# Seven block products instead of eight in the down products, and none in the first gate and up product of a layer

## The chip, the core and the metric

The kernel runs on one core of one Trainium2 chip. The core has TensorE (matrix products, PE in the rows), VectorE (DVE), ScalarE (ACT), GpSimd (POOL) and SyncE (SP, which issues the loads), and each runs its own instructions in order. The metric is the device time of one execution in microseconds, as the median of several runs.

## What is computed

Two layers of a transformer block on 256 tokens of width 2048, in float32. Each layer normalises x, runs three mixers (a gated recurrence, a differential attention and a latent attention), adds their projection to x, and then runs a gated feed-forward part of width 5632, which the change is about:

```python
h = rmsnorm(x, g_ffn[l])
x = x + (jax.nn.silu(h @ w_gate[l]) * (h @ w_up[l])) @ w_down[l]
```

with `w_gate`, `w_up` of 2048 x 5632 and `w_down` of 5632 x 2048. At the end stands one more `rmsnorm`.

## The kernel before

**Precision.** Each float32 operand is split into a high part, rounded to the format that TensorE multiplies in one pass (`F32R`), and a low part, the rest. A product takes three matmuls (`mm3`, lines 232 to 236): high x high, high x low, low x high. For weights, ScalarE makes the high part from the raw tile (L228) and VectorE the low part (L229), in `load_split`. Raw tiles (`wraw`) have six buffers of 128x1024; high and low parts (`whi`, `wlo`) have three each.

**Feed-forward.** The 5632 hidden columns are taken in eleven blocks f of 512, in three groups (0 to 3, 4 to 7, 8 to 10). For each block, `gate_up` computes gate and up for both halves of the tokens (t = 0, 1), and a step called `hidden`, which runs between the matmuls of whatever comes next, transposes the result on TensorE and splits it into `hTh` and `hTl`. After a group, two down products (cg = 0, 1, each of 1024 output columns) multiply the group's hidden activations by `w_down` and add to x. They are written with the general `gemm`: one k-tile of 128 rows and 1024 columns at a time, 12 matmuls each, four banks.

**Seven products.** `gate_up` goes over the 16 k-tiles in eight pairs. A pair is a 2x2 block problem: two token halves, two k-tiles, and gate and up. The first five pairs (`NORD = 5`) are plain: 2 x 2 x 2 = 8 block products, 24 matmuls. The last three pairs use a scheme with seven block products (21 matmuls). It needs sums of the left blocks (`xSh`, `xSl`, built once per layer by `build_xS`) and, per pair, sums of the weight blocks: V and W, four subtractions of 128x512 on VectorE (L340 to L343), which are then split like the weights G (gate) and U (up) themselves (L338, L339, L344 to L349). In the plain pairs the parts go to `whi` and `wlo`; in the seven pairs *all* parts go to two sets in the arena, a large scratch tile, so that the next product's first plain pairs can fill the three `whi` and `wlo` buffers meanwhile. The seven accumulators are C11, C22, C21, C12 and P1 (pool `acc`, five banks) and P5, P6, P7 (pool `aux`, three banks); at the end VectorE combines them (L360, L368, L369, L373, L375 to L378, L380).

**Order.** TensorE's order is that of the code. On VectorE, ScalarE and SP a scheduler orders the instructions ahead of time; whatever stands inside `tc.high_priority` is pulled forward as far as its inputs and buffers allow. A buffer of a pool is given to the next tile when the last reader of its old tile is through.

Of the kernel before, what the change touches and what calls it, by code (L numbers as in the profile page):

```python
# [16 lines left out]
ALU = mybir.AluOpType  # L17
# [20 lines left out]
NORD = 5  # L38
# [19 lines left out]
def body(ctx: ExitStack, tc: tile.TileContext, x_in, pos_in, pvec_in, lamv_in, cst_in, w_in, w_r, w_i, w_q_b,  # L58
# [27 lines left out]
    xSh = xt_p.tile([P, KD // 2 - NORD, 4, P], F32R, name="xSh")  # L86
    xSl = xt_p.tile([P, KD // 2 - NORD, 4, P], F32R, name="xSl")
# [52 lines left out]
    A_SET, SET = 64, 7168  # L140
# [157 lines left out]
    def gate_up(wg, wu, rs, sil):  # L298
# [4 lines left out]
        f_ = lambda v: v.bitcast(F32)  # L303
        C11, C22, C21, C12 = (acc() for _ in range(4))
        bank = {(0, 0): C11, (1, 1): C22, (0, 1): C21, (1, 0): C12}
        sub = {}
        u2, u3, o22 = (at(A_U + i * 512, 512) for i in range(3))
        tt = nc.vector.tensor_tensor

        def xp(k, t):  # L310
            return xTh[:, k, t * P:(t + 1) * P], xTl[:, k, t * P:(t + 1) * P]

        for p in range(NORD):
            ks = (2 * p, 2 * p + 1)
            hl = [load_split(w[2 * p * P:(2 * p + 2) * P], 2, (512,)) for w in (wg, wu)]
            for s, t in ((0, 0), (1, 1), (0, 1), (1, 0)):
                hi, lo = hl[s]
                for j, k in enumerate(ks):
                    mm3(bank[s, t], xp(k, t), (hi[:, j], lo[:, j]), p == 0 and j == 0,
                        (s, t) == (1, 1) and p == NORD - 1 and j == 1)  # L320
            yield
        with tc.high_priority(offset=AHEAD):
            nc.scalar.copy(o22, C22)
        P1 = acc()
        P5, P7, P6 = (aux() for _ in range(3))
        n = KD // 2
        for p in range(NORD, n):
            ks = (2 * p, 2 * p + 1)
            a = A_SET + p % 2 * SET
# [3 lines left out]
            gh, gl = at(a, 2, 512), at(a + 1024, 2, 512)  # L333
            uh, ul = at(a + 2048, 512), at(a + 2560, 512)
            vh, vl = at(a + 3072, 2, 512), at(a + 4096, 2, 512)
            wh, wl = at(a + 5120, 2, 512), at(a + 6144, 2, 512)
            with tc.high_priority(offset=AHEAD):
                nc.scalar.copy(fl(gh), fl(G))  # L338
                nc.scalar.copy(uh, U[:, 1])  # L339
# [5 lines left out]
                tt(ul, U[:, 1], f_(uh), ALU.subtract)  # L345
# [4 lines left out]
            first, end = p == NORD, p == n - 1  # L350
            q = p - NORD
            S = [(xSh[:, q, i], xSl[:, q, i]) for i in range(4)]
            mm3(P1, xp(ks[0], 0), (gh[:, 0], gl[:, 0]), first, end)
            if end:
                with tc.high_priority(offset=AHEAD):
                    nc.scalar.copy(sil[1], P1)
            mm3(C11, xp(ks[1], 0), (gh[:, 1], gl[:, 1]), False, end)
            if end:
                with tc.high_priority(offset=AHEAD):
                    tt(sil[0], sil[1], C11, ALU.add)  # L360
                    nc.scalar.activation(sil[0], sil[0], AF.Silu, scale=rs[:, 0:1])
            mm3(C12, S[3], (uh, ul), False, end)
            mm3(P5, S[0], (vh[:, 0], vl[:, 0]), first, end)
            mm3(P7, S[2], (vh[:, 1], vl[:, 1]), first, end)
            mm3(P6, S[1], (wh[:, 0], wl[:, 0]), first, end)
            if end:
                with tc.high_priority(offset=AHEAD):
                    tt(u2, sil[1], P6, ALU.add)  # L368
                    tt(u3, u2, P7, ALU.add)  # L369
            mm3(C21, xp(ks[1], 1), (wh[:, 1], wl[:, 1]), False, end)  # L370
            if end:
                with tc.high_priority(offset=AHEAD):
                    tt(sil[1], u3, C21, ALU.add)  # L373
# [32 lines left out]
    def build_xT(gname, l, k):  # L406
        with tc.high_priority(offset=AHEAD):
# [4 lines left out]
            if gname == "g_ffn" and k // 2 >= NORD:  # L412
                build_xS(l, k, ps)
# [648 lines left out]
```

## Time and profile before

| | |
|---|---|
| median of 3 runs | 2117.31 us (2115.34 to 2117.53) |
| the profiled execution | 2116.37 us |
| its span, first to last instruction | 2114.5 us |
| TensorE busy | 2078.1 us, 10,104 matmuls and transposes |
| VectorE busy | 1539.4 us |
| ScalarE busy | 1132.4 us |
| DMA | 391.16 MB, mean 185 GB/s |
| TensorE waits for VectorE's split L229 | 13.6 us in 23 waits |

Busy times are sums over the span; a matmul's duration overlaps the next one's, so TensorE's pace is read from the starts of its instructions. "Idle before, releaser" in a row tells how long the engine had waited and what ended that.

### The profile page before, as it was taken

To read this page: it belongs to the slowest core of one execution; us is meant where nothing else is said; L and a number is where in the kernel's file an instruction comes from. 1 tells how busy PE (TensorE), PEld (TensorE's weight loads), DVE (VectorE), ACT (ScalarE), POOL (GpSimd) and SP (SyncE) were. 2 spreads that over 40 slices of the span, in tenths; PEclk is the share of its full clock that TensorE was granted. 3 is DMA by queue.
4 is the path that set the end of the run, shared out by engine and by line. 5 is a ranking of instruction groups with operands and counts; after the bars stand their busy time and mean duration, and the time that the engine had idled before them with its cause. 6 is when DMAs were issued, how large, how long until landed. Compare 5 with 4: busy or idle time off the path is not lost.

```text
span 2114.5 us, 26989 instructions
## 1 busy us (share of the span) xinstructions
PE 2078.1 (98%) x10104; PEld 1738.2 (82%) x10104; DVE 1539.4 (73%) x2115; ACT 1132.4 (54%) x1541; POOL 14.9 (1%) x32
## 2 busy tenths in 40 slices
PE   8999999999999999999999999999999999999998
PEld 7898887787888888887898998877888888888786
DVE  5775757898469884698565756589884788758885
ACT  5764655555345553455447546465553555535554
POOL 0000000000000000000000000000000000000000
PEclk9999999999999999999999999999999999999999
DMA  7664555565656655565565645556556655666563
GB/s 244 170 181 135 163 176 154 185 223 189 191 168 205 205 197 192 175 211 199 173 191 156 195 124 175 177 158 206 189 199 191 196 195 174 210 193 204 180 216 133
DMA packets 183219, 391.16 MB, mean 185 GB/s; under 512 B 18960, under 2 KB 36384, under 8 KB 182960
## 3 DMA queue, kind: packets, MB, share of 16 engines
q1 hardware_dynamic: 183040, 389.36, 58.1%
q8 instruction: 79, 1.29, 0.3%
q14 instruction: 52, 0.43, 0.1%
q0 software_dynamic: 48, 0.09, 0.0%
HBM read 387.30 MB, written 2.10 MB: 184 GB/s over the span
## 4 chain that ended last, share of the span: by engine, by line
PE 59%; DVE 25%; DMA 9%; issue 4%; ACT 2%; DVEq 0%; SPq 0%; POOLq 0%; ACTq 0%; POOL 0%
PE acc L235 18%; PE acc L236 18%; PE acc L234 18%; DVE wlo L229 7%; DMA wraw<-in_w_up 5%; DVE arena L344 2%; DMA wraw<-in_w_gate 2%; DVE wraw L341 2%; DVE arena L349 2%; DVE wraw L342 2%; ACT whi L228 2%; PE aux L393 1%; DVE wraw L343 1%; DVE wraw L340 1%; DVE arena L345 1%
## 5 line engine op out<-in xcount | busy, mean ns | idle before, releaser
L229 DVE TENSOR_TENSOR wlo<-wraw,whi 128x1024 fp32r<-128x1024 f32 (+2 forms) x608 | 715.2, 1182 | 440.4 <-ACT whi L228 436.2
L228 ACT CAST whi<-wraw 128x1024 fp32r<-128x1024 f32 (+2 forms) x608 | 617.5, 1019 | 681.3 <-PE acc L236 532.7
L235 PE MATMUL acc<-wlo,xTh 128*128 128x512 f32 (+1 forms) x1200 | 467.1, 389 | 14.0 <-DVE wlo L229 13.6
L234 PE MATMUL acc<-whi,xTh 128*128 128x512 f32 (+1 forms) x1200 | 471.2, 393 | 0.0
L236 PE MATMUL acc<-whi,xTl 128*128 128x512 f32 (+1 forms) x1200 | 463.6, 386 | 0.0
L234 PE MATMUL acc<-whi,hTh 128*128 128x512 f32 (+1 forms) x992 | 388.9, 392 | 3.5 <-DVE arena L373 3.5
L236 PE MATMUL acc<-whi,hTl 128*128 128x512 f32 (+1 forms) x992 | 384.8, 388 | 0.0
L235 PE MATMUL acc<-wlo,hTh 128*128 128x512 f32 (+1 forms) x992 | 384.4, 388 | 0.0
L235 PEld LDWEIGHTS acc<-wlo,xTh 128*128 128x128 f32 x1200 | 225.5, 188 | 72.3 <-DVE wlo L229 30.0
L234 PEld LDWEIGHTS acc<-whi,xTh 128*128 128x128 f32 x1200 | 225.4, 188 | 44.0 <-ACT whi L228 0.5
L236 PEld LDWEIGHTS acc<-whi,xTl 128*128 128x128 f32 x1200 | 225.3, 188 | 44.0
L234 PEld LDWEIGHTS acc<-whi,hTh 128*128 128x128 f32 x992 | 186.4, 188 | 43.7 <-DVE arena L373 6.0
L236 PEld LDWEIGHTS acc<-whi,hTl 128*128 128x128 f32 x992 | 186.2, 188 | 38.0
L235 PEld LDWEIGHTS acc<-wlo,hTh 128*128 128x128 f32 x992 | 186.4, 188 | 36.2
L234 PE MATMUL acc<-xTh,whi 128*128 128x256 f32 x384 | 111.1, 289 | 1.7 <-ACT whi L228 1.2
L235 PE MATMUL acc<-xTl,whi 128*128 128x256 f32 x384 | 108.8, 283 | 1.9 <-DVE xTl L403 1.9
L236 PE MATMUL acc<-xTh,wlo 128*128 128x256 f32 x384 | 108.6, 283 | 0.5 <-DVE wlo L229 0.5
L348 ACT CAST arena<-wraw 128x1024 fp32r<-128x1024 f32 x66 | 69.6, 1054 | 61.4 <-DVE wraw L343 61.0
L346 ACT CAST arena<-wraw 128x1024 fp32r<-128x1024 f32 x66 | 69.5, 1053 | 49.8 <-DVE wraw L341 49.8
L344 DVE TENSOR_TENSOR arena<-wraw,arena 128x1024 fp32r<-128x1024 f32 x66 | 80.6, 1222 | 14.9 <-ACT arena L338 14.8
L338 ACT CAST arena<-wraw 128x1024 fp32r<-128x1024 f32 x66 | 69.3, 1050 | 23.8 <-DMA wraw<-in_w_gate 23.5
L349 DVE TENSOR_TENSOR arena<-wraw,arena 128x1024 fp32r<-128x1024 f32 x66 | 80.7, 1222 | 0.2
(230 smaller groups left out, 2523.1 us busy)
## 6 DMA issues: line engine op xcount, KB each, us to landing
wraw<-in_w_gate SPq DMA_DIRECT2D x176, 512.0 KB, 4.3
wraw<-in_w_up SPq DMA_DIRECT2D x176, 512.0 KB, 4.6
wraw<-in_w_down SPq DMA_DIRECT2D x176, 512.0 KB, 4.5
wraw<-in_w_out SPq DMA_DIRECT2D x64, 512.0 KB, 3.8
wraw<-in_w_in SPq DMA_DIRECT2D x48, 512.0 KB, 4.2
wraw<-in_w_in SPq DMA_DIRECT2D x48, 384.0 KB, 3.2
wraw<-in_w_in SPq DMA_DIRECT2D x32, 416.0 KB, 3.4
arena<-in_w_in SPq DMA_DIRECT2D x16, 384.0 KB, 7.4
```

The source lines that it names most:

```text
L228: nc.scalar.copy(hi[:, :n], raw[:, :n])
L229: nc.vector.tensor_tensor(lo[:, :n], raw[:, :n], hi[:, :n].bitcast(F32), ALU.subtract)
L234: nc.tensor.matmul(ps, a[0], b[0], start=start, stop=False)
L235: nc.tensor.matmul(ps, a[0], b[1], start=False, stop=False)
L236: nc.tensor.matmul(ps, a[1], b[0], start=False, stop=stop)
L338: nc.scalar.copy(fl(gh), fl(G))
L341: tt(V[:, 1], U[:, 1], U[:, 0], ALU.subtract)
L342: tt(W[:, 0], U[:, 1], V[:, 0], ALU.subtract)
L344: tt(fl(gl), fl(G), f_(fl(gh)), ALU.subtract)
L346: nc.scalar.copy(fl(vh), fl(V))
L348: nc.scalar.copy(fl(wh), fl(W))
L349: tt(fl(wl), fl(W), f_(fl(wh)), ALU.subtract)
```

## The change

`gate_up` becomes `paired`, which takes the left operands (`part`, `sums`), the two weight matrices and a function for the read-out (`ev`) as arguments. `gate_up` calls it as before, except that the first block of a layer (f = 0) passes no seven pairs: all eight are plain, and its four banks are read directly. `down` is new: it calls `paired` with the two halves of 512 columns of a down product in the places of gate and up, and with the pairs of hidden k-tiles on the left. Of eight pairs, 3, 4 and 5 are done last and by seven products. The third group has six pairs: its cg = 0 takes none, its cg = 1 takes pairs 3 and 4 in layer 0, and in layer 1 it stays with `gemm`. `hidden` builds the sums of hidden activations for these pairs (`build_sums`), into 3072 columns of the arena. That room comes from the sets: only V and W keep their parts in the arena (two sets of 4096), and the parts of G and U of a seven pair go to `whi` and `wlo`. `hidden` starts one pair earlier.

```diff
+SEVEN_X, SEVEN_H = (5, 6, 7), (3, 4, 5)
...
-            gh, gl = at(a, 2, 512), at(a + 1024, 2, 512)
-            uh, ul = at(a + 2048, 512), at(a + 2560, 512)
-            vh, vl = at(a + 3072, 2, 512), at(a + 4096, 2, 512)
-            wh, wl = at(a + 5120, 2, 512), at(a + 6144, 2, 512)
+            gh, uh = (whl_p.tile([P, CHUNK], F32R, name="whi").rearrange("p (a b) -> p a b", a=2) for _ in range(2))
+            gl, ul = (whl_p.tile([P, CHUNK], F32R, name="wlo").rearrange("p (a b) -> p a b", a=2) for _ in range(2))
+            vh, vl, wh, wl = (at(A_SET + (i % 2 * 4 + m) * 1024, 2, 512) for m in range(4))
...
+    def down(w, c, hT, order, seven, done):
...
+        def add_x(t, g, *vs):
+            a = x[:, t, c + g * 512:c + g * 512 + 512]
+            for v in vs:
+                tt(a, a, v, ALU.add)
+
+        def ev(stage, a, b=None, e=None):
+            if isinstance(stage, tuple):
+                g, t = stage
+                add_x(t, g, a)
+                done(t, g)
+            elif stage == "C22":
+                add_x(1, 1, a)
+            elif stage == "P1":
+                nc.scalar.copy(p1, a)
+            elif stage == "C11":
+                add_x(0, 0, p1, a)
+                done(0, 0)
+            elif stage == "P6":
+                tt(u2, p1, a, ALU.add)
+                tt(u3, u2, b, ALU.add)
+            else:
+                add_x(1, 0, a, u3)
+                done(1, 0)
+                tt(u2, u2, e, ALU.add)
+                add_x(0, 1, b, u2)
+                done(0, 1)
+                tt(u3, u3, e, ALU.add)
+                add_x(1, 1, u3)
+                done(1, 1)
...
+        return paired(w[:, c:c + 512], w[:, c + 512:c + 1024], order, seven, part, sums, ev)
...
+    def build_sums(hi, lo, ps, g):
+        a = at(A_U, 4, P)
+        if g is None:
+            nc.scalar.copy(a.rearrange("p a b -> p (a b)"), ps)
...
+        split_scaled(hi, lo, sm, None)
...
-                run(gate_up(w_gate[l][:, fs], w_up[l][:, fs], rs[0], sil))
+                run(gate_up(w_gate[l][:, fs], w_up[l][:, fs], rs[0], sil, SEVEN_X if f else ()))
...
-                    yield 2
+                    yield
...
+                            if 2 * f + k // 2 in SEVEN_H:
+                                build_sums(*hS(SEVEN_H.index(2 * f + k // 2)), ps, None)
...
+                if end and last and cg == 1:
+                    run(gemm(lambda k: hT[k], [(wd[:, c0:c0 + 1024], [(0, 512), (512, 512)])],
+                             [[k] for k in range(4 * (f1 - f0))], ev, last=3))
+                else:
+                    n = 2 * (f1 - f0)
+                    seven = SEVEN_H if n == 8 else SEVEN_H[:2] if cg else ()
+                    run(down(wd, c0, hT, [p for p in range(n) if p not in seven], seven, done))
```

The built programs show what this does to the order on VectorE. First place: a middle gate and up product (f = 5 of layer 0), where the last two plain pairs meet the first two seven pairs. `wlo` rows are low parts of plain tiles (and, in the changed kernel, of G and U), rows that write `wraw` are V and W, `hTl` is the split of `hidden`. Before:

```order
L229 TENSOR_TENSOR wlo_5734<-wraw_5731,whi_5733 128x1024
L345 TENSOR_TENSOR arena_3292<-wraw_5811,arena_3292 128x512
L400 TENSOR_TENSOR hTl_5605<-aux_5718,hTh_5604 128x512
L229 TENSOR_TENSOR wlo_5771<-wraw_5768,whi_5770 128x1024
L342 TENSOR_TENSOR wraw_5814<-wraw_5811,wraw_5813 128x512
L347 TENSOR_TENSOR arena_3292<-wraw_5813,arena_3292 128x1024
L343 TENSOR_TENSOR wraw_5814<-wraw_5809,wraw_5814 128x512
L229 TENSOR_TENSOR wlo_5777<-wraw_5774,whi_5776 128x1024
L349 TENSOR_TENSOR arena_3292<-wraw_5814,arena_3292 128x1024
L400 TENSOR_TENSOR hTl_5605<-aux_5761,hTh_5604 128x512
L340 TENSOR_TENSOR wraw_5852<-wraw_5850,wraw_5848 128x512
L341 TENSOR_TENSOR wraw_5852<-wraw_5850 128x512
```

With the change (V's low part is L351, W's two halves are L346 and L347, W's low part is L353, G's and U's are L348 and L349):

```order
L351 TENSOR_TENSOR arena_3292<-wraw_5927,arena_3292 128x1024
L481 TENSOR_TENSOR hTl_5719<-aux_5839,hTh_5718 128x512
L231 TENSOR_TENSOR wlo_5885<-wraw_5882,whi_5884 128x1024
L346 TENSOR_TENSOR wraw_5928<-wraw_5925,wraw_5927 128x512
L347 TENSOR_TENSOR wraw_5928<-wraw_5923,wraw_5928 128x512
L231 TENSOR_TENSOR wlo_5891<-wraw_5888,whi_5890 128x1024
L353 TENSOR_TENSOR arena_3292<-wraw_5928,arena_3292 128x1024
L348 TENSOR_TENSOR wlo_5931<-wraw_5923,whi_5929 128x1024
L344 TENSOR_TENSOR wraw_5970<-wraw_5968,wraw_5966 128x512
L345 TENSOR_TENSOR wraw_5970<-wraw_5968 128x512
L346 TENSOR_TENSOR wraw_5971<-wraw_5968,wraw_5970 128x512
L349 TENSOR_TENSOR wlo_5932<-wraw_5925,whi_5930 128x512
```

The low part of V, which stood behind W's first half, now stands ahead of it, and a 128x512 split of U that stood early is now the last row here, behind three rows (L344 to L346) of the second seven pair.

Second place: VectorE at the end of the first down product of the second group (`x` is the residual stream, `acc` and `aux` are banks, `arena2` holds partial sums). Before:

```order
L987 TENSOR_TENSOR x_84<-x_84,acc_6617 128x512
L229 TENSOR_TENSOR wlo_6946<-wraw_6943,whi_6945 128x1024
L987 TENSOR_TENSOR x_84<-x_84,acc_6621 128x512
L987 TENSOR_TENSOR x_84<-x_84,acc_6625 128x512
L987 TENSOR_TENSOR x_84<-x_84,acc_6629 128x512
L229 TENSOR_TENSOR wlo_6964<-wraw_6961,whi_6963 128x1024
```

With the change:

```order
L426 TENSOR_TENSOR x_84<-x_84,arena2_95 128x512
L231 TENSOR_TENSOR wlo_7133<-wraw_7130,whi_7132 128x1024
L426 TENSOR_TENSOR x_84<-x_84,acc_6782 128x512
L441 TENSOR_TENSOR arena2_95<-arena2_95,aux_6984 128x512
L426 TENSOR_TENSOR x_84<-x_84,acc_6784 128x512
L442 TENSOR_TENSOR arena2_95<-arena2_95,aux_6983 128x512
L231 TENSOR_TENSOR wlo_7139<-wraw_7136,whi_7138 128x1024
L426 TENSOR_TENSOR x_84<-x_84,arena2_95 128x512
L446 TENSOR_TENSOR arena2_95<-arena2_95,aux_6982 128x512
L426 TENSOR_TENSOR x_84<-x_84,acc_6785 128x512
L449 TENSOR_TENSOR arena2_95<-arena2_95,aux_6982 128x512
L426 TENSOR_TENSOR x_84<-x_84,arena2_95 128x512 x2
```

Four adds and two splits have become eleven adds and two splits; the second split, that of the next product's first up tile, stands behind the add of C21 (acc_6784) and that of u3 (L442).

## Rows read from the trace of the kernel before

**Rows 1.** The page, part 1: busy time, share of span, instructions; part 2: granted clock.

```profile
PE 2078.1 (98%) x10104; PEld 1738.2 (82%) x10104; DVE 1539.4 (73%) x2115; ACT 1132.4 (54%) x1541; POOL 14.9 (1%) x32
...
PEclk9999999999999999999999999999999999999999
```

**Rows 2.** Timeline of TensorE around one seven phase: start us, duration us, instruction, idle before.

```profile
716.52 0.39 PE L234 MATMUL acc<-arena,xTh 128*128 128x512 f32 x1
716.75 0.39 PE L235 MATMUL acc<-arena,xTh 128*128 128x512 f32 x1
...
730.80 0.39 PE L234 MATMUL acc<-whi,xTh 128*128 128x512 f32 x1
...
738.46 0.50 PE L235 MATMUL acc<-wlo,xTh 128*128 128x512 f32 x1 [0.47 <-DVE wlo L229]
```

**Rows 3.** Windows: stretch, length, then each engine's busy us and instructions, clock, DMA.

```profile
365.40:381.10 15.70, 14.61 (x65) 11.74 (x63) 14.63 (x23) 10.36 (x13) 0.00 (x0) 1.00 0.59 189
381.10:412.40 31.30, 29.19 (x130) 23.04 (x129) 26.66 (x33) 17.02 (x20) 0.00 (x0) 1.00 0.60 184
...
687.70:716.50 28.80, 28.62 (x129) 23.15 (x128) 24.05 (x31) 15.38 (x18) 0.00 (x0) 1.00 0.59 196
716.50:730.80 14.30, 14.30 (x64) 11.82 (x63) 14.30 (x17) 8.92 (x11) 0.00 (x0) 1.00 0.61 195
...
774.30:863.00 88.70, 88.22 (x393) 72.73 (x392) 48.14 (x49) 34.49 (x35) 0.00 (x0) 1.00 0.64 205
```

**Rows 4.** Waits of TensorE from 602 to 863 us: total us, times, longest.

```profile
PE acc L235 <- DVE wlo L229: 1.6, 4, 0.7
PE acc L234 <- DVE arena L373: 0.5, 1, 0.5
```

**Rows 5.** Timeline of VectorE in the plain pairs ahead of that seven phase.

```profile
704.11 0.69 DVE L340 TENSOR_TENSOR wraw<-wraw 128x512 f32<-128x512 f32 x1 [0.72 <-DMA wraw<-in_w_up]
704.72 0.68 DVE L341 TENSOR_TENSOR wraw<-wraw 128x512 f32<-128x512 f32 x1
...
708.79 0.69 DVE L342 TENSOR_TENSOR wraw<-wraw 128x512 f32<-128x512 f32 x1
```

**Rows 6.** Timeline of SP's DMA issues in the same stretch.

```profile
709.51 0.37 SPq L212 DMA_DIRECT2D wraw<-in_w_up  x1
```

**Rows 7.** Timeline of VectorE from the second seven pair to the next product.

```profile
714.50 0.69 DVE L340 TENSOR_TENSOR wraw<-wraw 128x512 f32<-128x512 f32 x1 [0.34 <-DMA wraw<-in_w_up]
...
718.65 1.22 DVE L347 TENSOR_TENSOR arena<-wraw,arena 128x1024 fp32r<-128x1024 f32 x1
719.79 1.22 DVE L349 TENSOR_TENSOR arena<-wraw,arena 128x1024 fp32r<-128x1024 f32 x1
...
726.21 1.22 DVE L349 TENSOR_TENSOR arena<-wraw,arena 128x1024 fp32r<-128x1024 f32 x1
...
732.86 0.69 DVE L373 TENSOR_TENSOR arena<-arena,acc 128x512 f32<-128x512 f32 x1
...
735.86 1.41 DVE L380 SCALAR_TENSOR_TENSOR arena<-arena,rs 128x512 f32<-128x512 f32 x2
737.19 1.22 DVE L229 TENSOR_TENSOR wlo<-wraw,whi 128x1024 fp32r<-128x1024 f32 x1
```

**Rows 8.** Timeline of VectorE at the end of a down product.

```profile
556.66 0.69 DVE L987 TENSOR_TENSOR x<-x,acc 128x512 f32<-128x512 f32 x1 [1.09 <-PE acc L236]
...
558.40 1.87 DVE L987 TENSOR_TENSOR x<-x,acc 128x512 f32<-128x512 f32 x3
```

**Rows 9.** Timeline of VectorE while it builds sums of normalised inputs.

```profile
352.33 0.28 DVE L431 TENSOR_TENSOR arena<-arena 128x128 f32<-128x128 f32 x1
352.54 0.28 DVE L429 TENSOR_TENSOR arena<-arena 128x128 f32<-128x128 f32 x1
```

**Rows 10.** DMA issues: tensor, count, KB each, median us to landing.

```profile
wraw<-in_w_up SPq DMA_DIRECT2D x176, 512.0 KB, 4.6
wraw<-in_w_down SPq DMA_DIRECT2D x176, 512.0 KB, 4.5
```

More of the change, by code (lines that the diff above doesn't have):

```diff
@@ L138, in body @@
     A_DQ = A_QT
[L140 removed]
+    A_SET = 64
+    A_HS = A_SET + 8192
     A_SIL = ARENA1
@@ L349, in gate_up @@
                 tt(fl(wl), fl(W), f_(fl(wh)), ALU.subtract)
[L350 to L353, printed above, removed]
+            first, end = i == 0, i == len(seven) - 1
+            S1, S2, S3, S4 = sums(p)
+            mm3(P1, part(e, 0), (gh[:, 0], gl[:, 0]), first, end)
             if end:
-                with tc.high_priority(offset=AHEAD):
-                    nc.scalar.copy(sil[1], P1)
@@ L357, in gate_up @@
-            mm3(C11, xp(ks[1], 0), (gh[:, 1], gl[:, 1]), False, end)
+                read("P1", P1)
+            mm3(C11, part(o, 0), (gh[:, 1], gl[:, 1]), False, end)
             if end:
[L359 to L364, printed above, removed]
@@ L365, in gate_up @@
-            mm3(P6, S[1], (wh[:, 0], wl[:, 0]), first, end)
+                read("C11", C11)
+            mm3(C12, S4, (uh[:, 1], ul[:, 1]), False, end)
+            mm3(P5, S1, (vh[:, 0], vl[:, 0]), first, end)
+            mm3(P7, S3, (vh[:, 1], vl[:, 1]), first, end)
+            mm3(P6, S2, (wh[:, 0], wl[:, 0]), first, end)
             if end:
-                with tc.high_priority(offset=AHEAD):
-                    tt(u2, sil[1], P6, ALU.add)
-                    tt(u3, u2, P7, ALU.add)
@@ L381, in gate_up, with gate, up, ev @@
-            yield
+                read("end", C21, C12, P5)
+            yield
+    def gate_up(wg, wu, rs, sil, seven):
+        tt = nc.vector.tensor_tensor
+        u2, u3, o22 = (at(A_U + i * 512, 512) for i in range(3))
+        def gate(t, v):
+            nc.scalar.activation(sil[t], v, AF.Silu, scale=rs[:, t:t + 1])
+        def up(t, v):
+            nc.vector.scalar_tensor_tensor(sil[t], v, rs[:, t:t + 1], sil[t], ALU.mult, ALU.mult)
+        def ev(stage, a, b=None, c=None):
+            if stage in ((0, 0), (0, 1)):
+                gate(stage[1], a)
+            elif stage in ((1, 0), (1, 1)):
+                up(stage[1], a)
+            elif stage == "C22":
+                nc.scalar.copy(o22, a)
+            elif stage == "P1":
+                nc.scalar.copy(sil[1], a)
+            elif stage == "C11":
+                tt(sil[0], sil[1], a, ALU.add)
+                gate(0, sil[0])
+            elif stage == "P6":
+                tt(u2, sil[1], a, ALU.add)
+                tt(u3, u2, b, ALU.add)
+            else:
+                tt(sil[1], u3, a, ALU.add)
+                gate(1, sil[1])
+                tt(u2, u2, c, ALU.add)
+                tt(u2, u2, b, ALU.add)
+                tt(u3, u3, c, ALU.add)
+                tt(u3, u3, o22, ALU.add)
+                up(0, u2)
+                up(1, u3)
+        def part(k, t):
+            return xTh[:, k, t * P:(t + 1) * P], xTl[:, k, t * P:(t + 1) * P]
+        def sums(p):
+            q = SEVEN_X.index(p)
+            return [(xSh[:, q, i], xSl[:, q, i]) for i in range(4)]
+        order = [p for p in range(KD // 2) if p not in seven]
+        return paired(wg, wu, order, seven, part, sums, ev)
```

109 lines of the change are left out of this document (58 added, 51 removed).

## Prediction

> **What bounds the kernel now.** I read the page first. TensorE is busy 98% of the span at the full granted clock, VectorE 73%, ScalarE 54% [rows 1]. A busy TensorE may still be stalling, so the next view is its timeline: three neighbouring matmuls of 512 columns start 0.227 us apart [rows 2]. That is the price of a matmul here. It makes a plain pair of k-tiles (24 matmuls) 5.44 us and a pair by seven products (21) 4.76 us, a gain of 0.68 us. Then the busy time by stage [rows 3]. In a gate and up product in the middle of a layer, five plain pairs take 28.8 us (27.2 of matmuls, 0.9 of transposes, the rest stall) and three seven pairs take 14.3 us, which is 63 x 0.227 exactly: no stall. But there VectorE is busy 14.30 of 14.30 us. In the down products it is busy 48 of 89 us. So TensorE is the bound in both, with VectorE directly behind it in one and with room in the other. Last, the waits of TensorE over a whole group of four products and its downs: only 2.1 us in 261 [rows 4], three quarters of it for a split by VectorE.
>
> **Where VectorE's chain starts and ends.** This carries the argument. In the product whose seven phase runs from 716.52 to 730.80 [rows 2], VectorE prepares the first seven pair during the plain pairs: V from 704.11, the first half of W until 709.48 [rows 5]. That half is the last reader of a raw buffer, and the up load of the *second* seven pair is issued at 709.51 [rows 6]. V of the second pair starts when it lands, at 714.50, 4.99 us later, and from there VectorE has no gap: the preparation of pairs two and three until 727.34, the read of C21 at 732.86, the last two of the read-out at 735.86, and then the split of the next product's second up tile, 737.19 to 738.41 [rows 7]. TensorE was waiting for that one: its matmul starts at 738.46, 0.47 us of it named as waiting for this split [rows 2]. The chain has no slack; whatever makes it later stalls TensorE by as much, once per product.
>
> **The change, part by part.**
>
> (a) *Matmuls.* Eight down products take three pairs by seven, layer 0's last one takes two: 26 pairs x 3 = 78 fewer. Two first products lose three pairs each: 18 more. Net 60 x 0.227 = **-13.6 us**, all on the path.
>
> (b) *The first product of a layer.* Its seven phase took 15.7 us where 14.3 is usual, and the plain phase behind it 31.3 where 28.8 is [rows 3]: 1.4 + 2.5 = 3.9 us of stall that came from VectorE being late with xT, the sums and three seven pairs at once. Without seven pairs that goes: two layers, **-7.8 us**. What is late next there is xT itself, as now. Ends: -4 and -8.
>
> (c) *The other 20 gate and up products.* The high and low parts of G and U move out of the arena into the three hi/lo buffers that the plain pairs use. The order shows two effects on VectorE's chain. First, between V and W of the first seven pair stands now the low part of V (128x1024) where a 128x512 stood. In a row, VectorE starts the next instruction 0.605 us after one of 512 and 1.137 us after one of 1024 [rows 5, 7], so W, the release and the load are 0.53 us later. Second, the low part of U of the first pair can be split only when the fifth pair's gate buffer is free, and stands now behind the *second* pair's V and W, in the chain: 0.605 us more. The chain is 1.14 us late at its end, the split of the next product's second up tile. 20 x 1.14 = **+22.7 us**. Queued behind it are only later splits, which have their time. The waits of each new bank I cost at nothing: C21's bank goes to C12 of the next product, first written 18 matmuls (4.08 us) after the end, and its read ends 2.75 us after it. Ends: if the load lands in 3.8 us instead of 5, V starts when the first pair is done, as early as before, and the term is 0; if it takes half a microsecond more, 33.
>
> [...]
>
> (d) *The down products.* VectorE gets three seven pairs' preparation, (4 x 0.605 + 0.605 + 3 x 1.137) - 2 x 1.137 = 4.16 us more each, and 12 read-out instructions in place of 4. It has the time: some 38 us of work in 41.5. The cost lies at the end. There the order puts the split of the next product's first up tile behind the adds of C21 and u3, and C21 is complete only at the product's end. On the clock of the seven phase: V of the second pair at -2.02 + 0.53 = -1.49; the preparation 12.84 + 0.605; the add of P1, a split, the add of C11 and u2, 2.95; so C21's add starts at 14.9, the product ends at 14.28. C21, u3 and the split end at 17.3; TensorE needs it at 14.28 + 6 x 0.227 + 0.23 = 15.87: 1.45 us of stall. Six adds later the next gate split ends at 22.1, wanted at 21.4: 0.7. So 2.15 us; eight of them, one more us for the short ninth, less the 0.5 us that four following products wait at that place now: **+16 us**. The down's read-out today is four adds, three of them in 1.87 us [rows 8]. Ends: 1.1 us each (only the three instructions behind the product's end), +8; 0.5 more each, +21.
>
> (e) *Sums of the hidden activations.* Four adds of 128 columns every 0.205 us and a split of 0.605 [rows 9]: 1.4 us. Fourteen builds stand in plain phases of gate and up, 20 us of VectorE; those phases have 28.8 - 24.05 = 4.75 us idle each, but mostly ahead of V. I take a third, **+6 us**; ends 0 and 20.
>
> (f) *At nothing:* the ScalarE copies (15.4 us busy in 28.8, hidden beside VectorE); the loads, as many and as large as before: w_down's, in rows of 1024 columns, take 4.5 us to land and w_up's, in rows of 512 as w_down's will be, 4.6 [rows 10]; SP waits on the same splits. Uncovered, a load late by 0.5 us is the upper end of (c). The transposes come one pair earlier, and the activations are ready.
>
> **Sum:** -13.6 - 7.8 + 22.7 + 16 + 6 = +23.3. On the profiled execution's 2116.4 us that is 2139.7; the median of the runs shown stands 0.9 above that execution, so **2140 us**.
>
> **Rivals.** *VectorE absorbs it (faster).* All its added work, some 140 us, lies under 2078 us of TensorE and it has 575 us idle; with loads landing in 3.8 us, (c) is 0, (d) 8 - 2 = 6, (e) 0: 2116.4 - 13.6 - 7.8 + 6 = 2101 us. For it: 27% idle, and stalls of 2 us in 261. Against: the idle time lies in the plain phases and downs, before the load that starts the chain, and the chain has no slack today. It decides if V of the second seven pair starts no later than 2 us ahead of the phase. [...] Chance 0.31.
>
> *They cancel.* The chain is late by half of what I count, (c) 11, (d) 8, (e) 2: 2116.4 - 0.4 = 2116 us. Nothing in the rows prefers it; 0.13.
>
> *The three buffers starve the seven phase.* If a seven pair's preparation could not run ahead at all, each phase would take VectorE's 3 x 6.43 = 19.3 us instead of 14.3: 29 phases, +145 us, about 2240. Against: G and U are read in the first three of seven products, so the buffers free early. 0.03, and beyond the range.
>
> *The change does not do what it says:* the matmuls of 512 columns in the order go from 7,684 to 7,624, so that is out.
>
> **Numbers.** A difference of 0.2% (4.2 us) is about what can be told from no change. Forecast with its bounds, slower: 0.53; starved 0.03; cancelling 0.13; absorbed 0.31. So faster 0.31, same 0.13, slower 0.56. The forecast's own range is 2122 to 2165 (the upper ends of (c) and (d), with part of (e)). For eight in ten the range must reach down through the absorbed case and a little under its 2101, since (d) may cost less there: 2097 to 2165.
>
> **What would show it.** In the profile after: 60 matmuls fewer at 0.227 us; the first seven phase of a layer gone and its neighbour at 28 us; plain phases behind a seven phase at about 30 us instead of 28.8 to 29.2, the wait being for the second up split; seven phases still near 14.3; the two downs of a group at about 88 us instead of 88.7, with waits of 1.5 us for the first up split of the following product. If plain phases stay at 29 us, (c) is wrong and the first rival holds; if seven phases grow to 19, the third.

## The result and the profile after

The changed kernel took 2138.57 us (median of four runs, 2136.63 to 2139.48) where the kernel before took 2117.36 (2115.34 to 2117.53): a ratio of 1.0101, with a 95% interval of 1.0084 to 1.0119. It is slower by 21 us, and the forecast was 2140. The profiled execution of each gives spans of 2134.5 and 2114.5 us, so +20.0 us are to be found in the trace.

The page of the changed kernel, part 1, and the costliest wait of TensorE, for the low part of a plain weight tile (L231 is now the split that was L229): us in total, times, longest.

```profile
PE 2073.5 (97%) x10044; PEld 1727.7 (81%) x10044; DVE 1672.4 (78%) x2381; ACT 1177.2 (55%) x1622; POOL 14.9 (1%) x32
```

```profile
PE acc L237 <- DVE wlo L231: 44.2, 48, 1.6
```

Beside [rows 1]: 60 instructions fewer on TensorE, 133 us more work on VectorE, and the waits for that split, 13.6 us before, are 44.2. Next the windows, which answer to [rows 3]; their columns are those.

```profile
334.77:380.21 45.44, 45.44 (x210) 37.59 (x208) 29.17 (x45) 28.14 (x42) 0.69 (x1) 1.00 0.64 185
380.21:408.37 28.16, 28.16 (x130) 23.30 (x128) 20.19 (x22) 13.94 (x16) 0.00 (x0) 1.00 0.47 136
...
688.85:718.68 29.83, 28.63 (x130) 23.15 (x128) 24.98 (x35) 14.26 (x17) 0.00 (x0) 1.00 0.50 166
718.68:732.96 14.28, 14.28 (x65) 11.83 (x63) 14.28 (x19) 11.02 (x13) 0.00 (x0) 1.00 0.71 232
732.96:763.89 30.93, 29.02 (x129) 22.99 (x128) 26.87 (x39) 15.50 (x20) 0.00 (x0) 1.00 0.50 165
512.12:600.81 88.69, 85.29 (x375) 69.10 (x374) 77.49 (x94) 44.88 (x50) 0.00 (x0) 1.00 0.58 188
600.81:630.93 30.12, 28.12 (x121) 22.30 (x120) 23.88 (x30) 11.91 (x13) 0.00 (x0) 1.00 0.57 182
```

In order: the first product of a layer (all plain, TensorE busy throughout); the plain phase behind it, 28.16 where 31.30 stood; a later product's plain phase, 29.83 where 28.80 stood; its seven phase, 14.28 as ever; the plain phase of the fourth product of the group, 30.93; the two downs of the first group, 88.69 (those of the second group took 88.70 before, with 18 matmuls, 4.1 us, more); and the plain phase behind them, 30.12. Taken from the first matmul of one product to that of the next, over the whole span:

| products | before, us | after, us | difference |
|---|---|---|---|
| first of a layer and the one behind it (2 x 2) | 185.3 | 175.8 | -9.5 |
| the 14 that follow a gate and up product | 606.4 | 624.1 | +17.8 |
| the 4 that follow a down | 168.0 | 177.3 | +9.3 |
| first downs of the groups with eight pairs (4) | 182.1 | 178.3 | -3.8, with 8.2 of matmuls less |
| second downs of these groups (4) | 174.1 | 178.8 | +4.7, with 8.2 of matmuls less |
| all else | | | +1.5 |

**One chain, followed.** The seven phase that begins at 718.68 is the one that began at 716.52 before. First VectorE (L344 V's first half, L351 the low part of V, L346 the first half of W, L348 the low part of G, L349 that of U), then SP, then TensorE:

```profile
706.11 0.69 DVE L344 TENSOR_TENSOR wraw<-wraw 128x512 f32<-128x512 f32 x1 [1.77 <-DMA wraw<-in_w_up]
...
708.53 1.23 DVE L351 TENSOR_TENSOR arena<-wraw,arena 128x1024 fp32r<-128x1024 f32 x1
...
712.01 0.68 DVE L346 TENSOR_TENSOR wraw<-wraw 128x512 f32<-128x512 f32 x1
...
715.15 1.21 DVE L348 TENSOR_TENSOR wlo<-wraw,whi 128x1024 fp32r<-128x1024 f32 x1
...
717.43 0.68 DVE L344 TENSOR_TENSOR wraw<-wraw 128x512 f32<-128x512 f32 x1
...
718.63 0.68 DVE L349 TENSOR_TENSOR wlo<-wraw,whi 128x512 fp32r<-128x512 f32 x1
```

```profile
712.72 0.37 SPq L214 DMA_DIRECT2D wraw<-in_w_up  x1
```

```profile
741.84 0.50 PE L237 MATMUL acc<-wlo,xTh 128*128 128x512 f32 x1 [1.62 <-DVE wlo L231]
```

V's low part (L351) stands ahead of W, and so do three adds of a build of sums (711.40 to 712.01); the load of the second pair is issued 5.96 us ahead of the phase (7.01 before, [rows 6]). V of the second pair starts 1.25 ahead (2.02 before), but not because of a wait for that load: from 706.11 on VectorE has no idle time. What stands shortly ahead of V now is the low part of G (715.15), made with the shared buffers only here. In the kernel before, it was made ahead of the *first* pair's V, and with buffers of its own, in e12 below, it is so again:

```profile
702.17 1.22 DVE L344 TENSOR_TENSOR arena<-wraw,arena 128x1024 fp32r<-128x1024 f32 x1 [0.58 <-ACT arena L338]
```

TensorE gets the second up split 23.16 us after the phase began, where it was 21.94 ([rows 2]). That is 1.22 us for the 1.14 of (c), but (c) had neither G's low part nor the sums in it.

**The end of a down.** The down ends at 600.81. VectorE: C21's add, u3, then the next product's first up split (L231), which TensorE waits for; below it the fourth pair, where V (L344) has waited for its load and stands ahead of two splits of plain tiles, and TensorE's two waits.

```profile
601.44 0.68 DVE L426 TENSOR_TENSOR x<-x,acc 128x512 f32<-128x512 f32 x1
602.04 0.68 DVE L442 TENSOR_TENSOR arena<-arena,aux 128x512 f32<-128x512 f32 x1
602.64 1.22 DVE L231 TENSOR_TENSOR wlo<-wraw,whi 128x1024 fp32r<-128x1024 f32 x1
...
619.03 0.69 DVE L344 TENSOR_TENSOR wraw<-wraw 128x512 f32<-128x512 f32 x1 [2.48 <-DMA wraw<-in_w_up]
...
620.24 2.35 DVE L231 TENSOR_TENSOR wlo<-wraw,whi 128x1024 fp32r<-128x1024 f32 x2
622.51 0.68 DVE L346 TENSOR_TENSOR wraw<-wraw 128x512 f32<-128x512 f32 x1
623.11 1.22 DVE L351 TENSOR_TENSOR arena<-wraw,arena 128x1024 fp32r<-128x1024 f32 x1
```

```profile
603.91 0.50 PE L237 MATMUL acc<-wlo,xTh 128*128 128x512 f32 x1 [1.35 <-DVE wlo L231]
...
621.51 0.50 PE L237 MATMUL acc<-wlo,xTh 128*128 128x512 f32 x1 [0.29 <-DVE wlo L231]
```

From matmul to matmul the first stall is 1.6 us over the pitch of 0.227, the one at the second pair 0.6, and a third, at 621.51, 0.6; the third was not in the forecast, and in the down that begins at 822.65 it was 1.5. The last two rows of VectorE matter further on: in this product, in whose plain pairs no `hidden` runs, V's low part (L351) stands *behind* W's first half.

### The profile page after: what moved, and what is told of

Same layout as the page of the kernel before. It is cut to its first block, busy times and chain, and to the rows that moved or that the text cites. A ratio compares the mean times of both kernels' runs of the same rounds, so it can differ in the third digit from the quotient of the medians.

```text
span 2134.5 us, 27278 instructions
## 1 busy us (share of the span) xinstructions
PE 2073.5 (97%) x10044; PEld 1727.7 (81%) x10044; DVE 1672.4 (78%) x2381; ACT 1177.2 (55%) x1622; POOL 14.9 (1%) x32
## 4 chain that ended last, share of the span: by engine, by line
PE 49%; DVE 36%; DMA 7%; issue 6%; ACT 2%; DVEq 0%; SPq 0%; POOLq 0%; POOL 0%; ACTq 0%
PE acc L237 15%; PE acc L238 15%; PE acc L236 14%; DVE wlo L231 9%; DMA wraw<-in_w_up 4%; DVE wlo L348 3%; DVE arena L351 3%; DVE arena L353 3%; DVE wraw L345 2%; DVE wraw L346 2%; ACT whi L230 2%; DVE wlo L349 2%; DVE wraw L344 2%; PE aux L474 2%; DVE x L426 2%
## 5 line engine op out<-in xcount | busy, mean ns | idle before, releaser
L230 ACT CAST whi<-wraw 128x1024 fp32r<-128x1024 f32 (+2 forms) x568 | 575.4, 1014 | 611.1 <-PE acc L238 464.3
L231 DVE TENSOR_TENSOR wlo<-wraw,whi 128x1024 fp32r<-128x1024 f32 (+2 forms) x568 | 662.5, 1177 | 314.6 <-ACT whi L230 309.9
L237 PE MATMUL acc<-wlo,xTh 128*128 128x512 f32 x1368 | 532.5, 389 | 28.7 <-DVE wlo L231 28.5
L236 PE MATMUL acc<-whi,xTh 128*128 128x512 f32 x1368 | 536.9, 392 | 0.0
L238 PE MATMUL acc<-whi,xTl 128*128 128x512 f32 x1368 | 528.9, 387 | 0.0
L237 PE MATMUL acc<-wlo,hTh 128*128 128x512 f32 (+1 forms) x836 | 327.2, 391 | 16.0 <-DVE wlo L231 15.7
L236 PE MATMUL acc<-whi,hTh 128*128 128x512 f32 (+1 forms) x836 | 328.5, 393 | 0.1
L238 PE MATMUL acc<-whi,hTl 128*128 128x512 f32 (+1 forms) x836 | 325.0, 389 | 0.0
L352 ACT CAST arena<-wraw 128x1024 fp32r<-128x1024 f32 x86 | 90.4, 1051 | 38.8 <-DVE wraw L347 38.6
L351 DVE TENSOR_TENSOR arena<-wraw,arena 128x1024 fp32r<-128x1024 f32 x86 | 104.8, 1219 | 0.0
L348 DVE TENSOR_TENSOR wlo<-wraw,whi 128x1024 fp32r<-128x1024 f32 x86 | 104.6, 1216 | 0.0
L353 DVE TENSOR_TENSOR arena<-wraw,arena 128x1024 fp32r<-128x1024 f32 x86 | 104.6, 1216 | 0.0
```

The costliest lines, as they stand in the source:

```text
L230: nc.scalar.copy(hi[:, :n], raw[:, :n])
L231: nc.vector.tensor_tensor(lo[:, :n], raw[:, :n], hi[:, :n].bitcast(F32), ALU.subtract)
L236: nc.tensor.matmul(ps, a[0], b[0], start=start, stop=False)
L237: nc.tensor.matmul(ps, a[0], b[1], start=False, stop=False)
L238: nc.tensor.matmul(ps, a[1], b[0], start=False, stop=stop)
L348: tt(fl(gl), fl(G), f_(fl(gh)), ALU.subtract)
```

## The experiments

Chips differ by a few us, so each kernel ran in turns with the kernel before on one chip (there 2110 to 2112 us). Kernels of different calls are compared by their ratios; the changed kernel's is 1.0101.

**e1: the first product alone.** The kernel before, with

```diff
-run(gate_up(w_gate[l][:, fs], w_up[l][:, fs], rs[0], sil))
+run(gate_up(w_gate[l][:, fs], w_up[l][:, fs], rs[0], sil, f > 0))
```

and a `gate_up` that makes all eight pairs plain for f = 0 and reads its four banks directly.

> The kernel before, with one part of the change alone: the first gate and up product of a layer takes none of its pairs by seven. Theory (VectorE's lateness in that product and the one behind it goes with its seven pairs): the two products together lose in each layer the 4.8 us that they lost in the changed kernel, 92.6 to about 87.9 us, so 2117.4 - 9.5 = about 2108 us, with 18 matmuls more. Rival (part of that came from the other code of the changed kernel, and the stall only moves to the next seven phase): 2113 to 2117 us.

Measured: 2098.59 against 2111.81 us, ratio 0.9941 (0.9929 to 0.9954), 13 us off. It is the fastest version of this study.

**e11: the kernel before, once more, with its trace.**

> The kernel before, unchanged, for its stages on the chip of these runs. If the 3.7 us that e1 won beyond the first two products of a layer are a chip on which loads land sooner, its plain phases behind a seven phase are 28.2 to 28.6 us here too, as in e1; if they came from the first products' lateness, they are 28.6 to 29.2 as in the profile before.

Measured: span 2107.0 (e1: 2095.3). The window of a later plain phase, first in e11, then in e1:

```profile
425.91:454.31 28.40, 28.40 (x129) 23.23 (x128) 24.19 (x31) 15.64 (x18) 0.00 (x0) 1.00 0.57 192
```

```profile
680.45:708.87 28.42, 28.42 (x130) 23.21 (x129) 24.20 (x31) 15.70 (x18) 0.00 (x0) 1.00 0.55 187
```

The first two products take 92.1 us per layer in e11 and 87.9 in e1, from matmul to matmul: 8.5 us over two layers. The later plain phases shown are 28.4 in both, where the profile before has 28.8 to 29.2: so far it is the chip. Of the 11.7 us between the spans 3.2 remain, spread over the later products; their cause stays open.

**e2: the shared buffers, without the new downs.** The changed kernel with `gemm` for every down and without `build_sums` in `hidden`. Beside e1 it has two things more: the shared buffers, and `hidden` one pair earlier.

> The changed kernel with plain down products as in the kernel before, and without the sums of the hidden activations: only the shared hi/lo buffers for G and U, and a first product without seven pairs, are left. Theory (term c: the shared buffers make VectorE's chain 1.14 us late in each of 20 gate and up products): 2108 + 23 = about 2131 us, and plain phases behind a seven phase near 30 us. Rival (the buffers cost nothing; the sums of the hidden activations and the down products cost it all): about 2108 us, and plain phases of 28.8 to 29.2 us.

Measured: 2119.56 us, ratio 1.0041 (1.0028 to 1.0053), 21.0 us over e1 on the same chip. TensorE's waits for the low part of a plain tile are 14.8 us in e2 and 2.4 in e1. One plain phase of e2 to set beside e1's at 680.45, and VectorE ahead of the second pair's V, first in e2 (L348 the low part of G, L344 V), then in e1 (L411 the split of `hidden`, L351 V):

```profile
684.54:713.88 29.34, 28.44 (x129) 23.23 (x128) 24.25 (x31) 13.61 (x16) 0.00 (x0) 1.00 0.50 171
```

```profile
710.69 1.22 DVE L348 TENSOR_TENSOR wlo<-wraw,whi 128x1024 fp32r<-128x1024 f32 x1
711.83 0.68 DVE L344 TENSOR_TENSOR wraw<-wraw 128x512 f32<-128x512 f32 x1
```

```profile
705.81 0.68 DVE L411 TENSOR_TENSOR hTl<-aux,hTh 128x512 fp32r<-128x512 f32 x1
706.41 0.69 DVE L351 TENSOR_TENSOR wraw<-wraw 128x512 f32<-128x512 f32 x1
```

VectorE has the same 24.2 us of work in both phases; it is late, not overloaded. Term (c) stands, near its size, and rival "absorbed" falls with it. How it comes about is not as forecast. V starts 2.05 us ahead of the phase in e2 and 2.46 in e1, and in both it follows the instruction before it without idle time: it does not wait for the load. In e2 a 128x1024 instruction stands ahead of it where in e1 a 128x512 stands. The rest of the 0.92 us lies behind V, where U's low part now stands in the second pair's chain.

**e4: the order at a down's end alone.** The changed kernel with

```diff
-                read("end", C21, C12, P5)
+                read("end", C21, C12, P5, ahead=AHEAD - late)
```

where `late` is 200 in `down` and 0 in `gate_up`: a smaller number puts the adds behind the next splits.

> The changed kernel with one change of order: at the end of a down product the splits of the next product's first pair stand ahead of the adds of C21, not behind them; the work is the same. Theory (term d: the split behind C21's add costs 1.45 us in each of nine products, and 0.5 where the second pair's follows): 9 x 1.45 = 13 us off, about 2126 us. Rival (the stall behind the downs is VectorE being late with everything, so another split is late in its place): 2135 to 2139 us.

Measured: 2119.78 us, ratio 1.0037 (1.0023 to 1.0051): 0.0064 under the changed kernel's, 13 us as forecast (7 to 20 with both intervals). VectorE at the same place, and the windows of two downs and of the plain phase behind them:

```profile
598.82 1.22 DVE L231 TENSOR_TENSOR wlo<-wraw,whi 128x1024 fp32r<-128x1024 f32 x1
...
600.56 1.22 DVE L231 TENSOR_TENSOR wlo<-wraw,whi 128x1024 fp32r<-128x1024 f32 x1
601.69 0.69 DVE L426 TENSOR_TENSOR x<-x,acc 128x512 f32<-128x512 f32 x1
```

```profile
511.43:598.19 86.76, 85.00 (x376) 69.17 (x374) 77.69 (x94) 44.93 (x50) 0.00 (x0) 1.00 0.57 193
598.19:626.26 28.07, 27.79 (x121) 22.37 (x120) 24.06 (x30) 11.93 (x13) 0.00 (x0) 1.00 0.61 197
```

C21's add comes behind both splits, the downs lose 1.9 us and the phase behind them 2.0. With the same work in another order, 13 us of term (d) go.

**e7: fewer sums.** The changed kernel with

```diff
-                            if 2 * f + k // 2 in SEVEN_H:
+                            if first and 2 * f + k // 2 in SEVEN_H:
```

> The changed kernel with the sums of the hidden activations built in the first group of four products alone; 10 of 16 builds are left out, and the later down products read the sums of the first group (that part of the computation is left out). Theory (term e: a third of 1.4 us each in the 14 products, here most of it in 9 of them): 4 us off, about 17 us over the kernel before. Rival 1 (the builds stand where VectorE is idle): no change, 21 us over the kernel before. Rival 2 (they stand in the chain with their whole 1.4 us, and the third product of the group pays for the raw buffer it holds up): 14 us off, about 7 us over.

Measured: 2125.52 us, ratio 1.0077 (1.0064 to 1.009), some 5 us under the changed kernel by the ratios; with both intervals that is 0 to 10. The expectation has the count wrong: the first add of a build runs 24 times in the changed kernel and 12 times here, six of them for the normalised inputs, so 12 of 18 builds are left out. Four of the 18, in the third groups, make sums that no product reads. The plain phase of the fourth product, 30.93 above, shows the cost plainly:

```profile
731.28:760.65 29.37, 28.46 (x130) 23.23 (x129) 24.27 (x31) 13.64 (x16) 0.00 (x0) 1.00 0.50 171
```

A plain phase that carries two builds pays 1.5 us for them, the others 0 to 0.7.

**e3 and e10: buffers of their own for the low part of G and both parts of U**, in the changed kernel (e3) and in e2 (e10):

```diff
-            gh, uh = (whl_p.tile([P, CHUNK], F32R, name="whi").rearrange("p (a b) -> p a b", a=2) for _ in range(2))
-            gl, ul = (whl_p.tile([P, CHUNK], F32R, name="wlo").rearrange("p (a b) -> p a b", a=2) for _ in range(2))
+            gh = whl_p.tile([P, CHUNK], F32R, name="whi").rearrange("p (a b) -> p a b", a=2)
+            b = A_GU + i % 2 * 2048
+            gl, uh, ul = at(b, 2, 512), at(b + 1024, 512), at(b + 1536, 512)
```

> The changed kernel whole, but the low part of G and both parts of U have buffers of their own in the arena again; only the high part of G shares with the plain pairs. In the order the low part of U leaves the chain of the second seven pair, the low part of V still stands ahead of W in the first. Theory (each is its own share of the 1.14 us: 0.605 for U, 0.53 for V): 20 x 0.605 = 12 us off, about 2126 us. Rival 1 (the sharing is the whole of term c): 23 us off, about 2116. Rival 2 (the load's landing sets the chain, not the buffers): no change, 2138.

> The kernel of e2 (plain down products, 8.7 us over the kernel before), with the low part of G and both parts of U in buffers of their own; of the seven pairs only the high part of G shares with the plain pairs. The low part of V still stands ahead of W in the first seven pair, as in e2; the low part of U is out of the second pair's chain, but the low part of G now stands inside it, behind W's first half. Theory (what VectorE's order puts into the chain is what counts, half of it by V's low part): 5 to 10 us of e2's 21 come back, about 0 to 4 us over the kernel before. Rival 1 (the shared buffers as such were it): all 21 come back, 13 under. Rival 2 (the high part of G, for whose buffer the scalar engine waits, holds it all up): nothing comes back, 9 over.

Measured: e3 2127.71 us, ratio 1.0081 (1.0067 to 1.0096), about 4 us under the changed kernel; e10 2115.48, ratio 1.0027 (1.0017 to 1.0037), 3 us under e2 and 18 over e1. In both the intervals overlap with those of the kernel compared, so neither gain is clear of none: e3 misses its theory and the first rival and can't be told from the second, e10 lies between its theory and the second rival. VectorE in e10 (L351 the low part of U, L353 that of V, L348 W's first half, L346 V) says why:

```profile
702.48 0.68 DVE L351 TENSOR_TENSOR arena<-wraw,arena 128x512 fp32r<-128x512 f32 x1
...
704.22 1.22 DVE L353 TENSOR_TENSOR arena<-wraw,arena 128x1024 fp32r<-128x1024 f32 x1
...
707.09 0.68 DVE L348 TENSOR_TENSOR wraw<-wraw 128x512 f32<-128x512 f32 x1
...
712.21 0.69 DVE L346 TENSOR_TENSOR wraw<-wraw 128x512 f32<-128x512 f32 x1 [0.22 <-DMA wraw<-in_w_up]
```

The low part of U has left the second pair's chain, but it now stands ahead of W *as well as* V's low part. W, the release and the load are later still, and V of the second pair starts 1.58 us ahead of the phase at 713.79, where in e2 it was 2.05. Here V does wait for its load. What was won at one place of VectorE's order went at another.

That holds only where `hidden` runs in the plain pairs. The products behind a seven phase, from matmul to matmul, against the same products of e1 (mean, us; e12 follows below, with buffers of their own for all parts):

| | e2 | e10 | e12 |
|---|---|---|---|
| f = 5 and 9 (4): no `hidden` in the plain pairs ahead of that phase | +0.67 | +0.05 | +0.06 |
| f = 2, 3, 6, 7 and 10 (10): `hidden` in them | +1.02 | +1.06 | +0.89 |

In the phases ahead of the four, V's low part stands behind W in all three kernels; ahead of the ten, it stands ahead of W. (Those four phases, of f = 4 and 8, differ in more than `hidden`: a down stands ahead of them.) With shared buffers the four lose about U's split (0.605 us), with buffers of their own next to nothing. So in the four products the buffers were it (0.67 us in e2, 0.05 in e10); in the ten, buffers gave nothing back (1.02 and 1.06), and the order in which VectorE took its work counted.

**e5, e6, e8: V and W in place.** Written into the raw buffers of G and U, they take no raw buffers of their own; the loads of the second and third pair can then start earlier. e5 is e4 with this, e6 has e3's buffers too, e8 is e1 with it. The low parts of G and U come ahead of V for it, and TensorE takes P7 and P6 ahead of P5:

```diff
-            V, W = (wraw_p.tile([P, CHUNK], F32, name="wraw").rearrange("p (a b) -> p a b", a=2) for _ in range(2))
...
                 tt(fl(gl), fl(G), f_(fl(gh)), ALU.subtract)
                 tt(ul[:, 1], U[:, 1], f_(uh[:, 1]), ALU.subtract)
+                tt(G[:, 0], U[:, 0], G[:, 0], ALU.subtract)
+                tt(U[:, 0], U[:, 1], U[:, 0], ALU.subtract)
+                tt(U[:, 1], U[:, 1], G[:, 0], ALU.subtract)
+                tt(G[:, 1], G[:, 1], U[:, 1], ALU.subtract)
```

> The kernel of e4 (8 us over the kernel before), with V and W written in place into the raw buffers of G and U once the low parts of G and U are split off; a seven pair then holds two raw buffers, not four, and VectorE's low parts of G and U stand ahead of V. The work is the same. Theory (the chain of raw buffer, load and VectorE's order sets the plain phases behind a seven phase): the loads of the second and third seven pair are issued earlier, the plain phases fall from 29.4 to 31 us towards 28.2, 20 gate and up and eight down products by about 1 us each: 25 us off, about 17 us under the kernel before. Rival (the three shared hi/lo buffers set it, which come free only as the matmuls go on; the low part of G ahead of V now waits for them too): no gain, 5 to 15 us over the kernel before.

> As e5, with the low part of G and both parts of U in buffers of their own as in e3: of the seven pairs only the high part of G shares with the plain pairs. Theory (raw buffers and loads set the plain phases): as e5 within 5 us. Rival (the shared hi/lo buffers set it): 10 us or more under e5.

> The kernel of e1 (13 us under the kernel before), with V and W in place as in e5, and all hi/lo parts of the seven pairs in buffers of their own as before. Theory (raw buffers and loads): the plain phases of 28.2 to 28.9 us go to the 28.2 of the product without a seven phase ahead of it, 20 x 0.3 = 6 us off, 19 us under the kernel before. Rival (VectorE's work, not its start, sets them; or the low part of U, which now stands ahead of V, delays it): no gain, 10 to 13 us under the kernel before.

Measured: e5 2286.22 us (ratio 1.0836, 1.0821 to 1.0851), e6 2248.83 (1.0662, 1.0647 to 1.0676), e8 2151.35 (1.0210, 1.0196 to 1.0224). All forecasts failed, and of the rivals only e6's came out, 10 us or more under e5: it is 37 under. VectorE in the seven phase of e8 that begins at 452.87 (L353 and L354 are steps of the third pair; L229 are splits of the *next* product):

```profile
459.96 1.22 DVE L229 TENSOR_TENSOR wlo<-wraw,whi 128x1024 fp32r<-128x1024 f32 x1
461.10 0.69 DVE L353 TENSOR_TENSOR wraw<-wraw 128x512 f32<-128x512 f32 x1
461.70 1.22 DVE L229 TENSOR_TENSOR wlo<-wraw,whi 128x1024 fp32r<-128x1024 f32 x1
462.84 0.68 DVE L354 TENSOR_TENSOR wraw<-wraw 128x512 f32<-128x512 f32 x1
463.44 1.22 DVE L229 TENSOR_TENSOR wlo<-wraw,whi 128x1024 fp32r<-128x1024 f32 x1
```

The scheduler puts three of the next product's splits (3.4 us) between the steps of a pair that TensorE is waiting for; the first stands 7.1 us into this phase, in e1 10.4 us into the one that begins at 708.87, behind the last pair's work. This phase takes 18.3 us in place of 14.3, part of it at a lower clock (0.92 on the mean). As far as these rows go, the scarce raw buffers had kept later work out of the chain; what the other two parts of the edit cost, no run tells.

**e9 and e12: put together.** Buffers of their own for all parts, one seven pair in each down of eight pairs, e1's first product and e4's order. In e9 it is pair 3; in e12

```diff
-SEVEN_X, SEVEN_H = (5, 6, 7), (3,)
+SEVEN_X, SEVEN_H = (5, 6, 7), (7,)
```

> Put together from what the runs favour: the first product of a layer takes no pair by seven (e1); all hi/lo parts of the seven pairs have buffers of their own, for which there is room when only one pair of a down product goes by seven (pair 3, in the eight down products with eight pairs); the splits of the next product stand ahead of the adds at a down's end (e4). Theory (the losses were the shared buffers and the order at the end of the downs, and both are gone): e1's 13 us under the kernel before, less 24 matmuls x 0.227 = 5.4, and some 2 back for the sums: about 16 us under it. Rival (any seven pair in a down product delays VectorE by more than the 0.68 us it saves): 5 to 12 us under it, more than e1.

> The kernel of e9 (1.3 us over the kernel before), with the last pair of the eight, pair 7, going by seven in a down product in place of pair 3. Its sums are then built in the first plain pairs of the first down product and not in the plain phase of a gate and up product; they are built four times and not six. Theory (the sums cost where VectorE's chain has no slack: in e9 the six products that build them have plain phases of 29.8 to 30.1 us where e1 has 28.2 to 28.5, and the four behind four of them lose half a microsecond): 6 x 1.5 + 4 x 0.5 = 11 us off, about 10 us under the kernel before, with plain phases of 28.2 to 28.5 us again. Rival (the sums cost as much in the down products): four builds x 1.5 stay, about 4 us under the kernel before.

Measured: e9 ratio 1.0006 (0.9997 to 1.0015), e12 0.9999 (0.9990 to 1.0008): no better than the kernel before, some 13 us behind e1, and no forecast or rival hit. The same plain phase, 29.95 us in e9, is in e12:

```profile
683.23:712.37 29.14, 28.49 (x129) 23.15 (x128) 24.12 (x29) 14.88 (x18) 0.00 (x0) 1.00 0.54 186
```

VectorE in it (L352 the low part of V, L347 W's first half, L349 the low part of G, L345 V of the second pair):

```profile
702.80 1.22 DVE L352 TENSOR_TENSOR arena<-wraw,arena 128x1024 fp32r<-128x1024 f32 x1
...
705.67 0.69 DVE L347 TENSOR_TENSOR wraw<-wraw 128x512 f32<-128x512 f32 x1
...
710.82 1.23 DVE L349 TENSOR_TENSOR arena<-wraw,arena 128x1024 fp32r<-128x1024 f32 x1 [1.38 <-ACT arena L343]
711.97 0.69 DVE L345 TENSOR_TENSOR wraw<-wraw 128x512 f32<-128x512 f32 x1
```

One build less gave this phase 0.8 us, yet it still is 0.7 over e1's 28.42. In e12 the low part of G stands ahead of V in the second pair and waits for ScalarE's copy, 1.38 us with VectorE idle; V starts 0.4 us ahead of the phase, in e1 2.5. So the sums are not what holds e12 up, and the theory of its expectation was wrong.

Shared buffers are not it either, since e12 has none. What e2, e9, e10 and e12 share and e1 has not is `hidden` one pair earlier. No run takes that alone, so its time isn't shown. Its effect on the order can be read from built programs: e1 built with `yield` for `yield 2` in `hidden`, and not run, has e12's order from the first pair's V to the second's in all twenty products, with V's low part ahead of W and G's low part ahead of the second pair's V in the sixteen that have `hidden` in their plain pairs; and e12 built with `yield 2` has e1's.

## Why the prediction was right

The direction, the time and the mechanism in the large came out: VectorE's chain had no slack, and work that was well under its idle time stalled TensorE because of its place. In the small, steps of (b), (c) and (f) were wrong, and one was missing in (d). Term by term, against the span's +20.0:

- **(a) Matmuls:** 60 fewer, -13.6 us as forecast; the pitch is unchanged (0.227 us).
- **(b) First product: mis-sized.** Forecast -7.8, in the trace -13.6 (the table's -9.5 with 4.1 us more of matmuls). I counted the stall in its seven phase (1.4) and in the plain phase behind it (2.5). The phase behind it went to 28.16, 3.1 us less. And its own plain phase, where VectorE already prepared the seven pairs, was 31.41 us before, some 2.3 more than the same five pairs take now (45.44 less three of 5.44), by a window of the kernel before:

```profile
333.99:365.40 31.41, 29.82 (x138) 23.94 (x137) 24.84 (x40) 22.24 (x37) 0.69 (x1) 1.00 0.46 133
```

  The sentence "What is late next there is xT itself, as now" was the wrong step: in that window TensorE's named waits, 1.6 us, are for splits of weight tiles (L229) and not for xT, and without the seven pairs it is busy for all of the 45.44 us.
- **(c) and (e) The chain and the sums: right, a little too large.** Forecast 22.7 + 6; in the trace 17.8 in the 14 products and 4.4 in the four first downs, 22.2 together. On one chip e2 gives 21.0 for (c), the earlier `hidden` included. How the 22.2 divide in the changed kernel no run tells exactly: e7 gives some 5 us for twelve of the eighteen builds, within 0 to 10. Of the two effects in (c), the second came out: U's low part in the second pair's chain. The first did not. W, the release and the load are later, but in the product followed, and in e2's, V waits for VectorE's own work: the low part of G, 1.137 us, stands there. In e2 it takes the place of a split of `hidden`, 0.605 us, and that the difference is again 0.53 is luck. The step in (f) that put the earlier transposes at nothing is not borne out either: with buffers of their own (e10, e12) the loss falls where `hidden` runs, in an order that goes with its earlier start. What that start costs by itself stays open.
- **(d) The downs' end: mis-sized.** Forecast 16, in the trace 9.3 in the products behind the downs, 12.9 in the second downs and 1.9 in the short one, 24.1 together. The two stalls I had came out, 1.6 for 1.45 and 0.6 for 0.7; the step missed the third, 0.6 to 1.5 us, where V waits for its load ahead of the plain splits. C21's add itself starts 14.91 us into the phase, for 14.9 forecast. e4 takes back 13 of it by order alone.

-13.6 - 13.6 + 22.2 + 24.1 = +19.1, and 0.9 lies elsewhere. So the total owes something to luck, in errors that cancel: (b) was 5.8 too small, (c) and (e) 6.5 too large, (d) 8.1 too small.

Of the rivals, *absorbed* fell with e2: 27% of idle time didn't help, since it lies ahead of the first pair's V and none is left from there on. The sign that the prediction named for it, V of the second pair 2 us ahead of the phase, doesn't decide: e2's V starts 2.05 ahead, and 0.92 us is lost all the same. *Starved* didn't happen in the changed kernel (seven phases of 14.28 to 14.38). In e5 phases of three seven pairs take 19.8 to 22.6 us, part of it at a lower clock (0.85 on the mean over the one of 22.6), and the kernel 176 us more than the one before.

## What to carry to other kernels

Where one engine feeds another in order and its chain ends just in time, read the place of every added instruction in that chain, not its share of idle time: about 1 us more in that chain cost 21 us over 20 products, and moving two splits ahead of a waiting add gave 13 back. Freeing a buffer need not shorten such a chain, since whatever now becomes ready early can be put in front of what is urgent. And of a change with several parts, try each alone: the part that left something out here (e1) was worth 13 us, and the rest lost more than twice that. That goes for the part that looks like nothing too: the one `yield` that starts `hidden` earlier was never taken alone, and the runs that carry it can't tell its cost from that of the other parts.

## What the runs showed of the hardware

TensorE's granted clock fell in the middle of e5, in a stretch (400 to 430.4 us) where the engine was busy for 26.24 of 30.40 us. Windows of 2 us in one seven phase of e5, the clock third from the end:

```profile
416.00:418.00 2.00, 0.70 (x4) 0.23 (x2) 2.00 (x4) 1.89 (x3) 0.00 (x0) 1.00 0.22 83
418.00:420.00 2.00, 0.50 (x1) 0.19 (x1) 2.00 (x4) 1.68 (x2) 0.00 (x0) 0.80 0.03 8
420.00:422.00 2.00, 1.91 (x5) 1.53 (x6) 2.00 (x4) 0.20 (x1) 0.00 (x0) 0.50 0.33 74
...
426.00:428.00 2.00, 2.00 (x11) 1.63 (x10) 0.78 (x2) 1.67 (x3) 0.00 (x0) 1.00 0.91 324
```

In two windows TensorE was busy 0.70 and 0.50 of 2 us; in the second the clock was 0.80, and 0.50 in the window behind. It stayed at 0.50 until 426 though TensorE was busy again (1.91, 2.00 and 2.00 of 2 us), and was 1.00 in the window from 426 on. While it lasted, the engine started 5 or 6 instructions in 2 us; from 426 on it started 11. So here some 6 slow microseconds came behind the stall, on top of its own length; both are part of e5's 176 us. Not every stall had them: from 410 to 412 TensorE was busy 0.73 of 2 us, and the clock stayed at 1.00 there and in the next three windows. What makes it fall these windows don't show. In the changed kernel the granted clock was 0.997 over the span.

A matmul of two `F32R` parts is one record in the traces, one of plain float32 operands two: in the kernel before, L816 runs 12 times at 256 columns (six heads, two layers) and has 24 records. At 141.07 us such a pair took 0.43 us to the next start; at 256 columns an `F32R` matmul took 0.12 (from 9.86 us on).
